# A hybrid decoder layer: the q, k and v projections as Strassen products over token halves

## The chip, the core and the metric

One core of a Trainium2 chip runs the whole program. It has a matmul engine (PE, with a separate weight load, PEld), three elementwise engines (VectorE or DVE, ScalarE or ACT, GpSimd or POOL), and SyncE (SP), which here issues nearly all transfers between DRAM and the core's two memories, SBUF and PSUM. Each engine executes its own instructions in order and waits for others by semaphores. The metric is device time in microseconds; less is better. The kernel before takes 2383.71 us, the median of three runs (2383.62 to 2387.13).

## What is computed

A decoder layer on x of 2048 tokens and 1024 channels, in float32. The normalised input h goes through one wide projection. One branch is a gated delta rule over chunks (its code is not touched). The other is causal attention in 12 combinations of 3 groups and 4 heads of 128 channels; the groups look at every token, every 4th or every 16th. Both branches are gated, projected, merged and added to x. What the change rewrites is the part from h to the three attention inputs, and the order of the attention blocks:

```python
h = rms_norm(x, norm_w[layer])
proj = h @ w_in[layer]
(dn_qkv, dn_z, dn_b, dn_a, swa_q, swa_k, swa_v, swa_z, gates) = jnp.split(proj, split_points, axis=-1)
...
sq = partial_rope(rms_norm(grp(swa_q), q_norm_w[layer][:, None, :]), cos, sin)
sk = partial_rope(rms_norm(grp(swa_k), k_norm_w[layer][:, None, :]), cos, sin)
sv = grp(swa_v)
for gi, (window, dilation) in enumerate(SWA_GROUPS):
    o_g, lse_g = dilated_window_attention(sq[:, :, gi], sk[:, :, gi], sv[:, :, gi], window, dilation)
```

Every float32 product is made of three: each operand is split into a rounded high part and the rest, its low part (`hh`, `hl` for h; `wh`, `wl` for weights), and high x high, high x low and low x high are added up in PSUM.

## The kernel before

**Data.** `hh` and `hl` stay in SBUF for the whole kernel, each [128 channels, 4 token groups of 512, 8 channel blocks, 512 tokens]. x is read twice, token-major for the row norms and channel-major (`xcol`) for the operand.

**Start.** `swa_first` (L368) loads the first unit's weights, clears `kq`, warms PE with 26 small matmuls and prepares the first 128 tokens of h; the other 15 pieces are prepared beside the first unit (`x_event`, `x_parts`).

**Units.** `swa_units` (L423) runs 12 units, one for each group and head, group 2 first. A unit projects 16 token blocks of 128 to 384 columns (q, k and v of its head). A block is one PSUM tile, 8 channel blocks x 3 matmuls at L238 to L240: 128 tokens are the loaded weights, 384 columns stream. A block is written in four quarters (`s_proj`); between them stand a third of an attention step (`att_slots`) and, from the block before, the normalisation (`s_norm`: square sums on ScalarE, the power -0.5 on GpSimd; `s_turn`: scaling on VectorE, rotation on GpSimd, the store to `rscr`). The next unit's weights are loaded and split from the seventh block on (`w384`).

**Attention.** 192 blocks wait in `self.att`, each with the step at which it starts. A step loads q, k, v of a block two steps ahead (`a_load`), transposes q and k (L290) and splits them into `kq`, then scores (L305 to L310), masks and takes the maximum (L312), exp (L317), transposes p (L324), multiplies by v (L332, L333) and stores to `oscr`. One block starts a step; a unit's blocks of groups 2 and 1 are added when the unit ends. What is left after the units is worked off beside the next matmuls by `att_background`, a third of a step every 6 matmuls.

**After.** `cunits` (L506) makes 36 column units for the other projections: 128 columns for all 2048 tokens, four PSUM tiles of 512 tokens, 24 matmuls each at L524 to L526. The first three (z) cover the rest of the attention; then come the delta rule and the final projections, which the change leaves alone.

**Order.** The engines' order is fixed by the code in the first part; from then on a scheduler places the instructions as it sees operands become ready, SP's too. Instructions that were written later can so stand earlier, the loads of weights above all.

## Time and profile before

| | |
|---|---|
| median of three runs | 2383.71 us |
| profiled execution, first to last instruction (span) | 2382.4 us |
| instructions in the profiled execution | 40700 |
| last matmul of the units (L240) | 1019.4 us |
| DMA over the span | 307.30 MB, 129 GB/s |

The span is the profiled execution's own time; 1.3 us lie between it and the median of the runs. A page of the profile gives each engine's busy time, the chain of work that ended last, and the costliest groups of instructions (line, engine, operation, output and inputs, count, busy us, mean ns of one, idle time before and what ended it). A matmul's duration includes its way through the array and overlaps the next one, so the cost of one in a row of many is the distance between two starts, which the timeline shows.

### The profile page before, as it was taken

How to read it: one execution, taken by the hardware profiler on the slowest of the kernel's cores; microseconds unless marked ns; L12 is line 12 of the kernel's file. 1: busy time of each engine (PE TensorE's matmuls, PEld its weight loads, DVE VectorE, ACT ScalarE, POOL GpSimd, SP SyncE). 2: the span in 40 equal slices, each digit the busy share in tenths (PEclk: the TensorE clock that was granted, in tenths of full speed). 3: DMA queues.
4: the chain of work that ended last, by engine and by line, in shares of the span. 5: the costliest groups of instructions: out<-in, count | busy, mean ns of one | idle time of the engine just before them, and what ended most of it. 6: DMA issues, size and time to landing. Idle time of an engine off the chain costs nothing.

```text
span 2382.4 us, 40700 instructions
## 1 busy us (share of the span) xinstructions
PE 2343.1 (98%) x13640; PEld 2133.7 (90%) x13640; DVE 1191.4 (50%) x2831; ACT 847.5 (36%) x3021; POOL 886.0 (37%) x1855
## 2 busy tenths in 40 slices
PE   8999999999999999999999999999999999999999
PEld 7899999999999999988878888888888878889988
DVE  5543344334334434344877775999344433454431
ACT  6433333344444434333666662111233313111110
POOL 6633333333333334310855671101233212433441
PEclk9999999999999999999999999999999999999999
DMA  8443344333333335233544443222577645554542
GB/s 283 158 116 111 107 123 121 95 103 112 110 97 112 108 91 128 86 91 92 142 121 130 116 115 116 69 73 75 193 209 203 182 151 157 164 178 156 149 140 75
DMA packets 378808, 307.30 MB, mean 129 GB/s; under 512 B 61352, under 2 KB 345320, under 8 KB 378216
## 3 DMA queue, kind: packets, MB, share of 16 engines
q1 hardware_dynamic: 378312, 304.64, 43.6%
q8 instruction: 108, 1.77, 0.3%
q14 instruction: 100, 0.82, 0.1%
q10 hardware_dynamic: 288, 0.07, 0.0%
HBM read 187.92 MB, written 116.69 MB: 128 GB/s over the span
## 4 chain that ended last, share of the span: by engine, by line
PE 85%; POOL 4%; DMA 4%; DVE 4%; ACT 2%; issue 2%; SPq 0%; POOLq 0%; ACTq 0%; DVEq 0%
PE mm L240 10%; PE mm L238 10%; PE mm L239 10%; PE mm L524 9%; PE mm L526 9%; PE mm L525 9%; PE mm L1054 2%; PE mm L1052 2%; PE mm L1053 2%; PE mm L1035 2%; PE mm L1037 2%; PE mm L1036 2%; PE po L333 2%; PE tp L290 2%; DMA gcb<-gcscr 1%
## 5 line engine op out<-in xcount | busy, mean ns | idle before, releaser
L238 PE MATMUL mm<-wh,hh 128*128 128x384 f32 (+1 forms) x1536 | 555.0, 361 | 6.3 <-ACT hh L131 2.9
L240 PE MATMUL mm<-wh,hl 128*128 128x384 f32 (+1 forms) x1536 | 519.7, 338 | 1.7 <-DVE hl L135 1.7
L239 PE MATMUL mm<-wl,hh 128*128 128x384 f32 (+1 forms) x1536 | 518.3, 337 | 0.7 <-DVE wl L79 0.6
L524 PE MATMUL mm<-hh,wh 128*128 128x512 f32 x1152 | 464.1, 403 | 0.0
L526 PE MATMUL mm<-hh,wl 128*128 128x512 f32 x1152 | 454.7, 395 | 0.0
L525 PE MATMUL mm<-hl,wh 128*128 128x512 f32 x1152 | 451.4, 392 | 0.0
L238 PEld LDWEIGHTS mm<-wh,hh 128*128 128x128 f32 x1536 | 290.2, 189 | 10.8 <-ACT wh L78 4.4
L239 PEld LDWEIGHTS mm<-wl,hh 128*128 128x128 f32 x1536 | 291.0, 189 | 1.7 <-DVE wl L79 1.1
L240 PEld LDWEIGHTS mm<-wh,hl 128*128 128x128 f32 x1536 | 289.3, 188 | 2.6 <-DVE hl L135 2.6
L526 PEld LDWEIGHTS mm<-hh,wl 128*128 128x128 f32 x1152 | 217.0, 188 | 46.9
L525 PEld LDWEIGHTS mm<-hl,wh 128*128 128x128 f32 x1152 | 217.4, 189 | 41.8
L524 PEld LDWEIGHTS mm<-hh,wh 128*128 128x128 f32 x1152 | 217.2, 189 | 42.0
L263 DVE SCALAR_TENSOR_TENSOR rec<-mm,st,wqk 128x128 f32<-128x128 f32 x384 | 116.7, 346 | 263.7 <-POOL st L255 244.2
L79 POOL TENSOR_TENSOR wl<-raw,wh 128x512 fp32r<-128x512 f32 (+1 forms) x73 | 104.6, 1445 | 382.3 <-ACT wh L78 382.0
L317 ACT ACTIVATE p<-sc,ol 128x128 f32<-128x128 f32 (+1 forms) x192 | 82.1, 428 | 316.8 <-DVE ol L315 273.0
L253 POOL TENSOR_SCALAR st<-st 128x2 f32<-128x2 f32 x192 | 38.0, 198 | 399.7 <-ACT rec L249 398.2
L249 ACT ACTIVATE rec<-mm 128x128 f32<-128x128 f32 x384 | 102.7, 273 | 185.0 <-PE mm L240 171.8
L1035 PE MATMUL mm<-oh,hh 128*128 128x256 f32 x512 | 143.9, 281 | 2.9 <-DVE gt L1039 2.9
L1037 PE MATMUL mm<-oh,hl 128*128 128x256 f32 x512 | 142.9, 279 | 0.0
L1036 PE MATMUL mm<-ol,hh 128*128 128x256 f32 x512 | 142.9, 279 | 0.0
L255 POOL TENSOR_TENSOR st<-st,mhalf 128x2 f32<-128x2 f32 x192 | 135.0, 703 | 16.0
L632 DVE SCALAR_TENSOR_TENSOR acc<-xr,cw,acc 128x512 f32<-128x512 f32 x144 | 122.4, 850 | 17.4 <-ACT acc L630 12.4
(244 smaller groups left out, 4332.0 us busy)
## 6 DMA issues: line engine op xcount, KB each, us to landing
rscr<-rec SPq DMA_DIRECT2D x192, 192.0 KB, 1.9
raw<-in_w_in_dram SPq DMA_DIRECT2D x138, 256.0 KB, 3.1
qk<-rscr SPq DMA_DIRECT2D x192, 128.0 KB, 2.2
gscr<-gt SPq DMA_DIRECT2D x64, 256.0 KB, 2.4
gt<-gscr SPq DMA_DIRECT2D x64, 256.0 KB, 3.5
oscr<-ol SPq DMA_DIRECT2D x192, 65.0 KB, 2.0
oc<-oscr SPq DMA_DIRECT2D x16, 780.0 KB, 5.3
v<-rscr SPq DMA_DIRECT2D x192, 64.0 KB, 2.0
```

What stands on the lines that cost most here:

```text
L238: nc.tensor.matmul(pr[:, :w], a, wh[:, k, :w], start=(k == 0), stop=False)
L239: nc.tensor.matmul(pr[:, :w], a, wl[:, k, :w], start=False, stop=False)
L240: nc.tensor.matmul(pr[:, :w], b, wh[:, k, :w], start=False, stop=(k == KT - 1))
L255: nc.gpsimd.tensor_tensor(out=st[:, 2:4], in0=st[:, 0:2], in1=self.mhalf[:, 0:2], op=ALU.pow)
L263: nc.vector.scalar_tensor_tensor(out=qk[:, j, :], in0=pr[:, j * P:(j + 1) * P], scalar=st[:, 2 + j:3 + j], in1=s["w"][2][:, j, :], op0=ALU ...
L524: nc.tensor.matmul(pr, wh[:, k, :], a, start=(k == 0), stop=False)
L525: nc.tensor.matmul(pr, wh[:, k, :], b, start=False, stop=False)
L526: nc.tensor.matmul(pr, wl[:, k, :], a, start=False, stop=(k == KT - 1))
L632: nc.vector.scalar_tensor_tensor(out=acc, in0=xr[:, j:j + 512], scalar=w[:, j:j + 1], in1=acc, op0=ALU.mult, op1=ALU.add)
L1035: nc.tensor.matmul(o, self.wbh[:, k, ms], oh[:, k, :], start=(k == b * 4), stop=False)
L1036: nc.tensor.matmul(o, self.wbh[:, k, ms], ol[:, k, :], start=False, stop=False)
L1037: nc.tensor.matmul(o, self.wbl[:, k, ms], oh[:, k, :], start=False, stop=(k == b * 4 + 3))
```

## The change

The projections are done for two token halves p of 1024 tokens. In a half, h is a 2 x 2 matrix of operands A (token half x channel half, each 512 x 512) and a pair of heads' weights a 2 x 2 matrix B (channel half x 256 columns). Strassen's method in Winograd's form makes the four blocks of the product from seven block products instead of eight, with the sums S1 to S4 of A and T1 to T4 of B. Eight operands (A and S) of one half, each high and low, fill `hh` and `hl`, but for A21, which no product uses: its place holds weights.

- `first_unit` prepares x, makes the sums on VectorE, splits them, and computes v of group 2 for all tokens in the plain way with 256 columns. All 16 operands go to DRAM (`opd`): those of half 1 (and A21) in pieces of 512 bytes a row as they are made, the others of half 0 by `save` in rows of 8 KB.
- 16 units follow (`self.seq`): 12 for q and k of two heads, four for v of a group. A unit is 7 products x 48 matmuls of 256 columns (L391 of the changed kernel). `evict` adds partial results held in SBUF, `consume` normalises (or stores, for v) two token blocks at a time. Where the half changes (after units 1, 6 and 12), each operand is replaced from DRAM after its last use; at the end the original layout of h is restored in the same way.
- Weights are loaded as B blocks; `w_sums`, `w_high`, `w_low` prepare a product's weights two products ahead, in a ring of four.
- A counter of six matmuls (a tick) times all of this. An attention step takes 4 ticks (`att_loop`); blocks are added as their units end, group 0 in two parts, for which each head loads and transposes one block again.
- PSUM and `rawp` are now allocated in two phases, with one buffer for the scores in the first. The mask step takes the scaled minimum, so one VectorE instruction a block falls away. In `cunits` the first unit takes its token groups in the order 2, 0, 1, 3.

```diff
+ORDER = [0, 4, 1, 5, 2, 6, 3, 7, 8, 12, 9, 13, 10, 14, 11, 15]
+OPS = ("A11", "A12", "A21", "A22", "S1", "S2", "S3", "S4")
+SLOT = {"A11": (2, 0), "A12": (2, 1), "A21": (3, 0), "A22": (3, 1), "S1": (0, 0), "S2": (0, 1), "S3": (1, 0), "S4": (1, 1)}
+HOME = {"S1": "A11", "S2": "A12", "S3": "A21", "S4": "A22"}
+PROD = (("A11", "a", True, "B11"), ("S2", "b", True, "T2"), ("A12", "a", False, "B21"), ("S3", "b", False, "T3"),
+        ("S1", "c", True, "T1"), ("A22", "b", False, "T4"), ("S4", "c", False, "B22"))
...
+    def slot(self, op):
+        n, h = SLOT[op]
+        return tuple(a[:, n, 4 * h:4 * h + 4, :] for a in (self.hh, self.hl))
...
+    def save(self, p, op):
+        for x, t in enumerate(self.slot(op)):
+            self.nc.sync.dma_start(self.opd_ap(p, op, x), t.bitcast(F32))
+
+    def restore(self, p, op, n, h):
+        for x, t in enumerate((self.hh, self.hl)):
+            self.nc.sync.dma_start(t[:, n, 4 * h:4 * h + 4, :].bitcast(F32), self.opd_ap(p, op, x))
...
+        if p or op == "A21":
+            for x, a in enumerate((h, l)):
+                self.nc.sync.dma_start(self.opd_ap(p, op, x, j), a.bitcast(F32))
...
+    def x_sums(self, m):
...
+        s1 = new("S1", a21, a22, ALU.add)
+        s2 = new("S2", s1, a11, ALU.subtract)
+        self.x_put(m, "S1")
+        new("S4", a12, s2, ALU.subtract)
+        self.x_put(m, "S2")
+        new("S3", a11, a21, ALU.subtract)
...
+    def x_put(self, m, op):
+        nc = self.nc
+        s = self.xsum.pop(op)
+        p, j = ORDER[m] // 8, ORDER[m] % 4
+        if p == 0:
+            h, l = (a[:, :, j * P:(j + 1) * P] for a in self.slot(op))
+        else:
+            h, l = self.xp.tile([P, 4, P], F32R, name="xh", bufs=4), s
+        nc.scalar.activation(h, s, AF.Copy)
+        nc.gpsimd.tensor_tensor(out=l, in0=s, in1=h.bitcast(F32), op=ALU.subtract)
+        if p:
+            nc.sync.dma_start(self.opd_ap(p, op, 0, j), h.bitcast(F32))
+            nc.sync.dma_start(self.opd_ap(p, op, 1, j), l)
...
+        for e in range(2):
+            self.ring.append(tuple(ap.tile([P, 4, 264], F32R, name=f"w{x}{e}", bufs=1) for x in "hl"))
+            self.ring.append(tuple(a[:, 3, 0:4, e * 256:(e + 1) * 256] for a in (self.hh, self.hl)))
...
+    def up_setup(self, up):
...
+        for j, nm in enumerate(("q_norm_w", "k_norm_w")):
+            nc.sync.dma_start(self.wqk[:, :, j, :], dr(self.i[nm], 0, [[0, P], [P, G], [1, P]]))
+        nc.sync.dma_start(self.rope, self.i["rope"])
...
+    def sp_setup(self, sp):
...
+        nc.sync.dma_start(self.mask, self.i["mask"])
         self.kq = sp.tile([P, 2, 3, P], F32R, name="kq", bufs=1)
         nc.vector.memset(self.kq[:, :, 0:2, :].bitcast(F32), 0.0)
...
+    def w_sums(self, gi):
...
+        if i == 1:
+            r[u, "T1"] = b11 = r.pop((u, "B11"))
+            sub(b11, r[u, "B12"], b11)
+            t2 = r[u, "T2"] = self.ap.tile([P, 4, 264], F32, name="wr", bufs=5)
+            sub(t2, r[u, "B22"], b11)
...
+    def w_ahead(self, gi):
...
+            if i == 5:
+                self.w_load(u + 1, "B11")
+                self.w_load(u + 1, "B12")
+            elif i == 6:
+                self.at(5, lambda: self.w_load(u + 1, "B22"))
+        if i == 0:
+            self.w_load(u, "B21")
...
+        self.w_sums(gi)
+        d = 2 if i in (1, 3, 5) else 0
+        self.at(d + 1, lambda: self.w_high(gi))
+        self.at(d + 3, lambda: self.w_low(gi))
...
-        for k in ks:
-            a, b = self.hh[:, t // 4, k, cs], self.hl[:, t // 4, k, cs]
-            nc.tensor.matmul(pr[:, :w], a, wh[:, k, :w], start=(k == 0), stop=False)
-            nc.tensor.matmul(pr[:, :w], a, wl[:, k, :w], start=False, stop=False)
-            nc.tensor.matmul(pr[:, :w], b, wh[:, k, :w], start=False, stop=(k == KT - 1))
...
+    def consume(self, u, tok, c, b, pr, add=None):
...
+        src, wait = pr, 0
+        if add is not None:
+            nc.vector.tensor_tensor(out=flat, in0=pr, in1=add, op=ALU.add)
+            src, wait = flat, 2
...
+                nc.scalar.activation(self.junk, src[:, j * P:(j + 1) * P], AF.Square, accum_out=st[:, j:j + 1])
+            nc.gpsimd.tensor_scalar(out=st[:, 0:4], in0=st[:, 0:4], scalar1=1.0 / P, scalar2=EPS,
+                                    op0=ALU.mult, op1=ALU.add)
+            nc.gpsimd.tensor_tensor(out=st[:, 4:8], in0=st[:, 0:4], in1=self.mhalf[:, 0:4], op=ALU.pow)
...
+                nc.vector.scalar_tensor_tensor(out=flat[:, s], in0=src[:, s], scalar=st[:, 4 + j:5 + j],
+                                               in1=self.wqk[:, g, j % 2, :], op0=ALU.mult, op1=ALU.mult)
...
+        self.at(wait + 6, scale)
+        self.at(wait + 8, turn)
...
+    def evict(self, u, i, b, pr):
...
+        if i == 0:
+            t = hold["p1", b] = self.up.tile([P, 512], F32, name="p1", bufs=2)
+            nc.scalar.activation(t, pr, AF.Copy)
+        elif i in (1, 3):
+            n = "u2" if i == 1 else "u3"
+            t = hold[n, b] = self.up.tile([P, 512], F32, name=n, bufs=2)
+            nc.vector.tensor_tensor(out=t, in0=pr, in1=hold["p1", b], op=ALU.add)
+        elif i == 2:
+            self.consume(u, 0, 0, b, pr)
+        else:
+            n, tok, c = {4: ("u3", 1, 1), 5: ("p1", 1, 0), 6: ("u2", 0, 1)}[i]
+            self.consume(u, tok, c, b, pr, hold.pop((n, b)))
...
+    def unit(self, u):
...
+        for i, (op, tgt, first, _) in enumerate(PROD):
+            gi = 7 * u + i
+            self.w_ahead(gi + 2)
+            if first:
+                acc[tgt] = [self.ps.tile([P, 512], F32, name="mm", bufs=4) for _ in range(2)]
+            ah, al = self.slot(op)
+            wh, wl = self.W.pop(gi)
+            for b in range(2):
+                pr = acc[tgt][b]
+                for jj in range(2):
+                    cs = slice((2 * b + jj) * P, (2 * b + jj + 1) * P)
+                    o = pr[:, jj * 256:(jj + 1) * 256]
+                    for k in range(4):
+                        mm = lambda x, y, **kw: nc.tensor.matmul(o, x, y, skip_group_check=True, **kw)
+                        mm(ah[:, k, cs], wh[:, k, :], start=first and jj == 0 and k == 0, stop=False)
+                        mm(ah[:, k, cs], wl[:, k, :], start=False, stop=False)
+                        mm(al[:, k, cs], wh[:, k, :], start=False, stop=(k == 3))
+                        if k % 2:
+                            self.hook()
+                self.evict(u, i, b, pr)
+            if nxt is None:
+                if op in HOME:
+                    self.restore(1 - p, HOME[op], *SLOT[op])
+                if i == 6:
+                    self.restore(p, "A21", *SLOT["A21"])
+            elif nxt != p:
+                self.restore(nxt, op, *SLOT[op])
...
+    def first_unit(self, pinned):
...
+            for m in range(1, 16):
+                t = 8 * m
...
+                    on(t - 18, lambda m=m: (self.x_stat(m), self.x_nat(m + 1)))
+                    on(t - 14, lambda m=m: self.x_diag(m))
+                on(t - 11, lambda m=m: event(m))
+                on(t - 7, lambda m=m: (self.x_high(m, 0), self.x_high(m, 1)))
+                on(t - 6, lambda m=m: (self.x_low(m, 0, nc.vector), self.x_low(m, 1, nc.gpsimd)))
+                if m % 2:
+                    on(t - 5, lambda m=m: self.x_sums(m))
+                    on(t - 1, lambda m=m: self.x_put(m, "S4"))
+                    on(t + 2, lambda m=m: self.x_put(m, "S3"))
+            on(80, lambda: [self.w_load(0, n) for n in ("B11", "B12", "B22", "B21")])
+            for j, op in enumerate(o for o in OPS if o != "A21"):
+                on(76 + 6 * j, lambda op=op: self.save(0, op))
...
+    def att_loop(self, ph):
+        if self.att_on:
+            self.att_slots(self.step, ph)
+            if ph == 2:
+                self.step += 1
+            self.at((1, 2, 1)[ph], lambda: self.att_loop((ph + 1) % 3))
...
-                                       scalar=-3e38, scale=1.0, op0=ALU.add, op1=ALU.max, accum_out=ol[:, 129:130])
-        nc.vector.tensor_scalar(out=ol[:, 128:129], in0=ol[:, 129:130], scalar1=-SCALE, scalar2=None, op0=ALU.mult)
+                                       scalar=3e38, scale=-SCALE, op0=ALU.add, op1=ALU.min, accum_out=ol[:, 128:129])
...
-        nc.scalar.activation(p[:, lo:hi], sc[:, 256 + lo:256 + hi], AF.Exp, bias=ol[:, 128:129], scale=SCALE,
+        nc.scalar.activation(p[:, lo:hi], sc[:, 256 + lo:256 + hi], AF.Exp, bias=ol[:, 128:129], scale=-1.0,
                              accum_out=ol[:, 129:130])
...
+    def att_add(self, h, g, items, step):
+        for u, has, pre in items:
+            at = max(step + 6, self.att[-1]["at"] + 1) if self.att else step + 6
...
+            self.att.append(dict(g=g, h=h, i=u, at=at, slot=self.aslot, pre=pre, prev=self.att[-1] if has else None))
...
+        self.scb = 1
+        self.seq = [(0, "qk", 2, (0, 1)), (0, "qk", 2, (2, 3)), (1, "qk", 2, (0, 1)), (1, "qk", 2, (2, 3)),
+                    (1, "v", 1, None), (1, "qk", 1, (0, 1)), (1, "qk", 1, (2, 3)),
+                    (0, "v", 1, None), (0, "qk", 1, (0, 1)), (0, "qk", 1, (2, 3)),
+                    (0, "v", 0, None), (0, "qk", 0, (0, 1)), (0, "qk", 0, (2, 3)),
+                    (1, "v", 0, None), (1, "qk", 0, (0, 1)), (1, "qk", 0, (2, 3))]
...
+        self.first_unit(pinned)
+        xst.close()
+        self.up_setup(pool(ust, "up"))
+        self.sp_setup(pool(sws, "sp", "right"))
+        with pinned(False):
+            self.att_on = True
+            self.at(1, lambda: self.att_loop(0))
+            for u in range(len(self.seq)):
+                self.unit(u)
+                self.att_ready(u)
+            self.att_on = False
+            self.flush()
+        ust.close()
+        ast.close()
+        psa.close()
+        pst = ExitStack()
+        self.ps = self.ctx.enter_context(tc.tile_pool(name="ps", bufs=2, space=PSUM, **tile_))
```

**VectorE at the passage to the units.** `kq` is the buffer of split q and k of the attention; `[waits DMAHW...]` names the transfers' semaphores. Before, its clearing is among the first instructions:

```order
L1212 UNCONDITIONAL_BRANCH
L60 MEMSET mhalf 128x8
L159 MEMSET kq 128x2x256
L88 MEMSET ones 128x128
L193 TENSOR_TENSOR wl<-raw,wh 128x384
```

Now it stands between the weight sums of unit 0 (L259; the first row of it makes T1 and T2, the next T3), and waits for two transfers; L282 behind it makes the low part of T2:

```order
L259 TENSOR_TENSOR wr<-wr 128x4x256 [waits DVE_49] x2
L235 MEMSET kq 128x2x256 [waits DMAHW1_49,DMAHW0_49]
L259 TENSOR_TENSOR wr<-wr 128x4x256
L282 TENSOR_TENSOR hl<-wr,hh 128x4x256 [waits Activation_49]
L366 TENSOR_TENSOR u_1853<-mm,p_1797 128x512 [waits PE_49,Activation_49]
L366 TENSOR_TENSOR u_1880<-mm,p_1823 128x512 [waits PE_49,Activation_49]
L259 TENSOR_TENSOR wr<-wr 128x4x256 [waits DVE_49]
L334 SCALAR_TENSOR_TENSOR rec<-mm,st,wqk 128x128 [waits PE_49,DMAHW5_49,Activation_49,Pool_49]
```

The clearing moved from the kernel's start to behind the work of the first unit, because the buffer lies where that unit's buffers lay.

**SP at the same place.** Before, the norm weights `wqk` and the rotation table are loaded among the first pieces of x:

```order
L102 DMA xc<-in_xcol_dram 128x1024
L97 DMA xt<-in_x_dram 128x1024 x2
L409 DMA wqk<-in_q_norm_w_dram 128x128
L409 DMA wqk<-in_k_norm_w_dram 128x128
L410 DMA rope<-in_rope_dram 128x512
```

Now they are issued behind the last stores of operands (`opd1S...`) and of v:

```order
L206 DMA opd1S_123<-xh 512x1x128
L207 DMA opd1S_124<-xsum 512x1x128
L500 DMA vs_92<-rec 128x512
L206 DMA opd1S_121<-xh 512x1x128
L207 DMA opd1S_122<-xsum 512x1x128
L226 DMA wqk<-in_q_norm_w_dram 128x3x128
L226 DMA wqk<-in_k_norm_w_dram 128x3x128
L227 DMA rope<-in_rope_dram 128x512
```

The loads moved behind 58 MB of other transfers.

**PE at the end of the units.** Before, the column units (L524) follow the last projection (L240) directly:

```order
L240 MATMUL mm<-wh,hl 128x384
L524 MATMUL mm<-hh,wh_13346 128x512
L525 MATMUL mm<-hl,wh_13346 128x512
L526 MATMUL mm<-hh,wl_13347 128x512
L524 MATMUL mm<-hh,wh_13346 128x512
```

Now attention (L523 to L565) and transposes of the delta rule's decay (L693, L746) stand between the last projection and the first column matmul (L659):

```order
L556 MATMUL tp<-ident,p 128x128 x2
L542 MATMUL sc<-kq 128x256
L543 MATMUL sc<-kq 128x256
L564 MATMUL po<-v,pT 128x128
L565 MATMUL po<-v,pT 128x128
L523 MATMUL tp<-ident,qk 128x128 x2
L659 MATMUL mm<-hh,wh_14446 128x512
L660 MATMUL mm<-hl,wh_14446 128x512
```

Three blocks of attention moved ahead of the column units, and of the 39 blocks left there 24 stand together further on, with 63 column matmuls among them (4 of 20 before, with 15).

535 lines of the change are left out of this document (260 added, 275 removed).

## The prediction

> **What bounds the kernel now.** I read the page first, then the PE timeline in three places, then the windows and the DMA view.
>
> ```profile
> span 2382.4 us, 40700 instructions
> PE 2343.1 (98%) x13640; PEld 2133.7 (90%) x13640; DVE 1191.4 (50%) x2831; ACT 847.5 (36%) x3021; POOL 886.0 (37%) x1855
> ...
> PE 85%; POOL 4%; DMA 4%; DVE 4%; ACT 2%; issue 2%; SPq 0%; POOLq 0%; ACTq 0%; DVEq 0%
> PE mm L240 10%; PE mm L238 10%; PE mm L239 10%; PE mm L524 9%; PE mm L526 9%; PE mm L525 9%; PE mm L1054 2%; PE mm L1052 2%; PE mm L1053 2%; PE mm L1035 2%; PE mm L1037 2%; PE mm L1036 2%; PE po L333 2%; PE tp L290 2%; DMA gcb<-gcscr 1%
> ```
>
> PE is busy 98% of the span and carries 85% of the chain that ended last; the projection lines L238 to L240 are 30% of it. The next rows say whether anything else ends last in that stage (columns: PE, PEld, DVE, ACT, POOL busy with instruction counts, granted clock, DMA share, GB/s).
>
> ```profile
> 0.00:60.00 60.00, 48.72 (x255) 46.04 (x256) 35.37 (x110) 38.60 (x101) 38.70 (x77) 0.91 0.86 282
> 60.00:110.00 50.00, 44.39 (x249) 42.32 (x248) 28.00 (x82) 24.88 (x87) 36.87 (x83) 1.00 0.51 166
> 110.00:1000.00 890.00, 888.69 (x5626) 882.11 (x5625) 350.00 (x1246) 347.31 (x1544) 339.55 (x1026) 1.00 0.38 109
> ```
>
> From 110 to 1000 us PE idles 1.3 us in 890, the others are under 40% busy, and DMA is at 0.38. So in this stage a matmul taken away is time won. In the first 110 us PE idles 11.3 + 5.6 = 16.9 us and DMA is already at 0.86: there, more transfers may cost.
>
> **Term 1, the matmuls.** A matmul's own duration overlaps the next one's, so I take start-to-start spacing.
>
> ```profile
> 600.25 0.34 PE L239 MATMUL mm<-wl,hh 128*128 128x384 f32 x1
> ...
> 601.98 0.34 PE L240 MATMUL mm<-wh,hl 128*128 128x384 f32 x1
> ...
> 40.11 0.34 PE L238 MATMUL mm<-wh,hh 128*128 128x384 f32 x1
> ...
> 42.04 0.34 PE L240 MATMUL mm<-wh,hl 128*128 128x384 f32 x1
> ...
> 2199.76 0.28 PE L1036 MATMUL mm<-ol,hh 128*128 128x256 f32 x1
> ...
> 2206.36 0.28 PE L1035 MATMUL mm<-oh,hh 128*128 128x256 f32 x1
> ```
>
> 384 columns: 10 steps from 600.25 to 601.98 give 173 ns, 11 from 40.11 to 42.04 give 175.5; I use 174. 256 columns, with the same kind of operands in the last stage: 56 steps in 6.60 us, 117.9 ns. Before: 12 units x 16 blocks x 24 = 4608 x 0.174 = 801.8 us. Changed: 768 in the first V unit and 16 x 7 x 48 = 5376, together 6144 x 0.1179 = 724.4 us. The eight columns for beta and decay ride on 384 matmuls in both. **-77 us.** The attention blocks keep their matmuls; four extra blocks, one a head, only transpose: 0.14 (599.85 to 599.99 under Term 3) and some 0.1 for the slower matmul behind them. **+1**.
>
> **Term 2, the stores of the split operands: the term that decides.** The change writes all 16 operands, high and low, to DRAM: 33.6 MB. The queue up to the last of them also holds x twice (16.8), two units' weights (4.2) and 15 V blocks (3.9): 58 MB ahead of the query and key norm weights, in SP's order. Two instructions wait for that. VectorE's clearing of `kq` waits for two DMA lanes, which I take for two among the last sixteen small stores (55.6 to 57.7 MB into the queue). Queued behind it on VectorE are T3's subtraction and the low part of T2, and PE waits for that low part in the second product of unit 0. The normalisation L334 waits for `wqk`, which stands right behind the stores; that lands about when the products after the first wait are done, so it is not counted again. How fast does the queue move?
>
> ```profile
> 10.00:20.00 10.00, 6.38 (x25) 5.52 (x25) 6.59 (x17) 6.33 (x13) 6.24 (x7) 0.66 1.07 357
> ...
> 1700.00:1900.00 200.00, 198.99 (x1333) 173.56 (x1333) 79.41 (x253) 68.56 (x267) 55.48 (x169) 1.00 0.68 194
> ...
> L79 DVE TENSOR_TENSOR wl<-raw,wh 128x512 fp32r<-128x512 f32 x66 | 45.8, 695 | 110.7 <-ACT wh L78 108.5 <-DMA oscr<-ol 2.1
> ```
>
> The busiest ten microseconds moved 357 GB/s at a share of 1.07, that is 334 at one. The stage at 1700 us, with many short rows like those in the small stores (512 B each), gives 194/0.68 = 285. The first 60 us gave 282. I take 334: 55.6 to 57.7 MB take 166 to 173 us, from 2 us on, so the wait ends at about 172, and clearing, subtraction and split (1.4 each for twice the 512 elements of L79, an estimate) add 3. Without the wait PE would be there at 16.9 (the idle time of today, kept) + 4.9 (warm-up matmuls, busy in the first row) + 816 x 0.118 + 1 = 119 us. **+56 us**; at 357 and the nearer store 42, at 285 and the farther one 88.
>
> The Trainium skill, "DMA: Bandwidth & Descriptors", section "Specifications", speaks against the change here: it gives an HBM limit of about 358 GB/s a core, and by it, as an estimate, the term would be 45 to 50. It also gives 435 GB/s as the fabric's ceiling; the trace has passed the first figure for some microseconds (the row under the rivals), so I don't take it for a wall.
>
> **Term 3, the pace inside the units.** A block of attention now has 24 matmuls of 118 ns (2.83 us) beside it, not 24 of 174.
>
> ```profile
> 599.85 0.38 PE L290 MATMUL tp<-ident,qk 128*128 128x128 f32 x2
> 599.99 0.42 PE L238 MATMUL mm<-wh,hh 128*128 128x384 f32 x1
> ...
> 605.42 0.42 PE L238 MATMUL mm<-wh,hh 128*128 128x384 f32 x1
> ...
> L249 ACT ACTIVATE rec<-mm 128x128 f32<-128x128 f32 x384 | 102.7, 273 | 185.0 <-PE mm L240 171.8 <-POOL rec L274 7.0 <-DMA rscr<-rec 4.6
> L78 ACT ACTIVATE wh<-raw 128x512 fp32r<-128x512 f32 x138 | 87.0, 633 | 70.6 <-PE mm L525 66.1 <-DMA raw<-in_w_in_dram 4.3 <-POOL hl L135 0.3
> L317 ACT ACTIVATE p<-sc,ol 128x256 f32<-128x256 f32 x108 | 51.2, 474 | 177.6 <-DVE ol L315 177.6
> L297 ACT ACTIVATE kq<-tp 128x256 fp32r<-128x256 f32 x128 | 49.3, 385 | 65.0 <-PE tp L290 64.5
> L298 DVE TENSOR_TENSOR kq<-tp,kq 128x256 fp32r<-128x256 f32 x128 | 54.3, 424 | 49.4 <-ACT kq L297 49.4
> L326 ACT ACTIVATE pT<-tp 128x256 f32<-128x256 f32 x108 | 41.6, 385 | 37.2 <-PE tp L324 37.2
> ```
>
> One step today is 5.43 us, of which 1.25 are attention on PE; it becomes 4.08. ScalarE then has per step four squares (0.27), exp (0.47 and its sum), two evictions (0.39) and half a weight rounding (1.27 for twice the 512 elements, an estimate): 3.1 of 4.08. Between the transposes and the score that uses them stand 12 matmuls and one transpose, 1.8 us, where 18 wide ones stood (3.1 us); the chain inside is 0.39 on ScalarE and 0.42 on VectorE with hand-offs. It fits unless another item is ahead on either engine. VectorE is over its time only in the last product of a unit (two adds, eight scalings, two weight sums and two blocks: about 8.9 us in 8.2). Nine units have both; I take 0.9 us each, **+8**; nothing at the low end (the 1.3 us in 890 of today), 36 if half of the 126 blocks there lose 0.6 us.
>
> **Term 4, the switches of halves.** Three times 14.7 MB come back, 44 us at 334 GB/s, in a unit of 40 to 57 us; each operand has a whole unit between its release and its next use. Weights and attention loads queue behind 2 MB pieces of 6 us. **+5** (0 to 15).
>
> **Term 5, from the units to the z columns.**
>
> ```profile
> 1019.39 0.34 PE L240 MATMUL mm<-wh,hl 128*128 128x384 f32 x1
> 1019.57 0.39 PE L524 MATMUL mm<-hh,wh 128*128 128x512 f32 x1
> 1019.79 0.40 PE L525 MATMUL mm<-hl,wh 128*128 128x512 f32 x1
> ...
> 1018.38 0.38 SPq L284 DMA_DIRECT2D v<-rscr  x1
> ...
> L255 POOL TENSOR_TENSOR st<-st,mhalf 128x2 f32<-128x2 f32 x192 | 135.0, 703 | 16.0
> L263 DVE SCALAR_TENSOR_TENSOR rec<-mm,st,wqk 128x128 f32<-128x128 f32 x384 | 116.7, 346 | 263.7 <-POOL st L255 244.2 <-DMA v<-rscr 15.5 <-DMA oscr<-ol 3.8
> L271 POOL TENSOR_TENSOR t<-rec,rope 128x64 f32<-128x64 f32 x192 | 64.8, 338 | 146.0 <-DVE rec L263 135.4 <-DMA qk<-rscr 6.4 <-DMA v<-rscr 2.6
> ...
> raw<-in_w_in_dram SPq DMA_DIRECT2D x138, 256.0 KB, 3.1
> ```
>
> Today the z matmuls follow without a gap, because their weights were loaded before. Now SP issues that load behind the last normalised block: add 0.7 (as L79), squares 1.1, power 0.9 for four columns, four scalings 1.4, eight rotations 2.4, some nine issues at 0.4, landing 3.1, rounding 0.6: 13.8 us and hand-offs of 1. Three blocks of attention (3.8 us) cover part: **+11** (6 to 15).
>
> **Term 6, the drain.**
>
> ```profile
> 1108.71 0.39 PE L333 MATMUL po<-v,pT 128*128 128x128 f32 x2
> ...
> 1118.38 0.39 PE L333 MATMUL po<-v,pT 128*128 128x128 f32 x2
> ```
>
> By the order, 39 blocks are left behind the units, not 20, and 24 of them, not 4, have only 2 to 4 z matmuls beside them. Those four took 9.67 us with 15 z matmuls of 0.22: 2.42 a block, 0.3 of it idle. 24 x 0.33 = **+8** (4 to 20). What follows is unchanged.
>
> **The sum:** -77 + 1 + 56 + 8 + 5 + 11 + 8 = +12 on the profiled 2382.4, so 2394; the median 2383.7 lies 1.3 above that span: **2396 us**. Low ends give -24, high ends +98.
>
> **The rivals.** *Faster: the stores run like the long transfers.* The DMA view of 1675 to 1710 us gives the rate in 40 slices:
>
> ```profile
> GB/s 274 26 0 0 0 0 165 160 134 444 502 393 449 412 468 393 468 431 393 487 342 337 286 28 0 0 45 238 239 325 301 353 347 207 209 244 302 369 355 237
> ```
>
> Here two transfers of 2 MB held about 440 for ten microseconds. Half of the new stores are long rows too. At 400 overall the wait ends at 146 instead of 172, Term 2 is 30, and with the other terms in the lower half (3, 2, 9, 6) the sum is -26: 2358. It decides from about 360 GB/s, where the sum passes zero with the other terms as forecast. Against it: the other half are 512 B rows, and the 285 above. *Slower: the pace of attention becomes the bound,* VectorE and ScalarE being late for each score by 0.3 us in 126 blocks: +38 for 8, 2426. For it the slack of 1.8 us instead of 3.1; against it ScalarE at three quarters. *The matmuls don't get shorter,* because a weight load is the limit at 256 columns:
>
> ```profile
> L1036 PEld LDWEIGHTS mm<-ol,hh 128*128 128x128 f32 x512 | 95.8, 187 | 0.3
> ```
>
> If each cost its 187 ns, 6144 x 0.069 = +424. The spacing of 117.9 with the same loads speaks against it.
>
> **How the numbers follow.** Forecast 0.53, faster rival 0.30, pace 0.15, weight loads 0.02. A measurement of this kernel can tell about 0.2%, 5 us. Of the forecast 0.10 and of the faster rival 0.03 lie within that: faster 0.27, same 0.13, slower 0.60. The forecast's own range is 2378 to 2430. The range given goes down into the faster rival and up past the pace rival, 2352 to 2450: below and above it I leave 0.1 each. As cases of both signs hold much, the sign is weak.
>
> **What would show it.** Term 1: L391 spaced 118 ns, PE busy about 75 us less. Term 2: PE idle for 40 to 90 us before unit 0's second or fifth product, released by VectorE, with DMA near a share of one from 60 to 170 us; if PE is through unit 0 by 160 us, the term is wrong and the kernel is faster. Term 3: idle at the scores, released by VectorE. Term 5: one gap before the first z matmul, released by ScalarE's rounding. Term 6: blocks 2.2 to 2.5 us apart. A gap in the units above 3 us that a restored operand ends would make Term 4 wrong.

## The result: 5.4% slower

| | before | changed |
|---|---|---|
| median of 4 runs | 2384.08 us | 2513.62 us (2512.80 to 2515.84) |
| ratio, 95% interval | | 1.0543 (1.0528 to 1.0557) |
| span of the profiled execution | 2382.4 us | 2513.9 us |

The forecast was 2396, with a range to 2450: the sign was right, the size wrong by 118 us. First the page of the changed kernel (same parts as those shown of before):

```profile
span 2513.9 us, 43806 instructions
...
PE 2330.1 (93%) x15184; PEld 2106.3 (84%) x15184; DVE 1389.9 (55%) x2882; ACT 959.6 (38%) x2976; POOL 1066.5 (42%) x1754
...
PE 58%; DMA 6%; POOL 5%; DVE 3%; ACT 3%; issue 2%; SPq 0%; POOLq 0%; ACTq 0%; DVEq 0%
```

PE is busy 13 us less than before (2330 for 2343), not some 75 less as forecast, and idle 184 us instead of 39. The chain that ended last has only 58% on PE (85% before); DMA has 6% and GpSimd (POOL) 5%, 4% each before. The shares listed add up to 77%, so the chain does not account for the whole span. The windows say where the time went. They are cut at the changed kernel's stages: first unit (two rows), the 16 units, the passage from the last product to the first column matmul, the rest; then before, cut at 110 us and at its last L240 (columns as in the prediction).

```profile
0.00:110.00 110.00, 80.00 (x540) 77.20 (x541) 62.53 (x135) 55.48 (x118) 56.14 (x63) 0.86 0.86 269
110.00:191.80 81.80, 39.29 (x289) 38.66 (x287) 23.55 (x51) 22.06 (x47) 25.16 (x23) 0.75 1.00 346
191.80:1080.80 889.00, 830.32 (x6755) 815.85 (x6756) 507.44 (x1261) 423.67 (x1458) 504.64 (x988) 0.97 0.57 178
1080.80:1109.70 28.90, 7.87 (x33) 5.23 (x32) 9.43 (x31) 6.71 (x28) 11.05 (x37) 0.59 0.83 236
1109.70:2513.90 1404.20, 1372.67 (x7573) 1169.36 (x7572) 786.89 (x1408) 451.70 (x1326) 469.50 (x646) 0.99 0.47 135
```

```profile
0.00:110.00 110.00, 93.11 (x502) 88.36 (x503) 63.37 (x191) 63.48 (x187) 75.57 (x160) 0.95 0.70 229
110.00:1019.50 909.50, 908.19 (x5752) 901.50 (x5751) 357.55 (x1273) 354.65 (x1574) 346.52 (x1048) 1.00 0.38 108
1019.50:2382.40 1362.90, 1341.83 (x7390) 1143.81 (x7388) 770.51 (x1368) 429.37 (x1260) 463.95 (x648) 1.00 0.46 135
```

The loss is in every stage: 72 us idle in the first unit, 59 in the units (1.3 before), 21 in the passage, 10 more than before in the rest. In the changed kernel the granted clock (the third number from the end) is under 1 in every stage, and lowest where the idle share is largest. The waits of PE in the changed kernel name the releasers (us in all, times, longest):

```profile
PE tp L140 <- ACT dg L136: 58.4, 11, 17.1
PE tp L556 <- ACT p L549: 19.2, 22, 4.4
PE mm L391 <- POOL wl L282: 15.2, 3, 5.2
PE tp L693 <- DVE s L721: 15.2, 1, 15.2
PE tp L823 <- DVE kT L772: 15.1, 5, 10.4
PE tp L523 <- DMA qk<-qks: 13.9, 8, 4.5
PE mm L391 <- ACT wh L275: 9.3, 1, 9.3
PE mm L391 <- POOL hl L282: 6.4, 2, 4.7
```

L140 spreads the norms of the next 128 tokens in the first unit; L556 and L523 are attention; L391 waits for weights (the 9.3 us stand ahead of unit 0's first product); L693 and L823 stand in the passage and behind the drain. The second product of unit 0, where the forecast had put its wait, does not appear.

### The profile page after: what moved, and what is told of

It is laid out like the page before. It is cut to its first block, busy times and chain, and to the rows that moved or that the text cites. A ratio compares the mean times of both kernels' runs of the same rounds, so it can differ in the third digit from the quotient of the medians.

```text
span 2513.9 us, 43806 instructions
## 1 busy us (share of the span) xinstructions
PE 2330.1 (93%) x15184; PEld 2106.3 (84%) x15184; DVE 1389.9 (55%) x2882; ACT 959.6 (38%) x2976; POOL 1066.5 (42%) x1754
## 4 chain that ended last, share of the span: by engine, by line
PE 58%; DMA 6%; POOL 5%; DVE 3%; ACT 3%; issue 2%; SPq 0%; POOLq 0%; ACTq 0%; DVEq 0%
PE mm L391 10%; PE mm L659 8%; PE mm L661 8%; PE mm L660 8%; PE mm L1189 2%; PE mm L1187 2%; PE mm L1188 2%; PE mm L1170 2%; PE mm L1172 2%; PE mm L1171 2%; DMA gcb<-gcscr 2%; DMA qk<-qks 2%; PE tp L523 1%; PE po L565 1%; POOL kql L863 1%
## 5 line engine op out<-in xcount | busy, mean ns | idle before, releaser
L659 PE MATMUL mm<-hh,wh 128*128 128x512 f32 x1152 | 466.9, 405 | 0.0
L391 PE MATMUL mm<-wh,hh 128*128 128x256 f32 x896 | 274.2, 306 | 9.3 <-ACT wh L275 9.3
L391 PE MATMUL mm<-wl,hh 128*128 128x256 f32 x896 | 259.4, 290 | 16.1 <-POOL wl L282 15.2
L391 PE MATMUL mm<-hh 128*128 128x256 f32 x896 | 270.1, 301 | 1.9 <-ACT hh L275 1.9
L391 PE MATMUL mm<-hl,hh 128*128 128x256 f32 x896 | 254.6, 284 | 6.4 <-POOL hl L282 6.4
L391 PE MATMUL mm<-wh,hl 128*128 128x256 f32 x896 | 259.3, 289 | 0.0
L391 PE MATMUL mm<-hh,hl 128*128 128x256 f32 x896 | 254.5, 284 | 0.0
L659 PEld LDWEIGHTS mm<-hh,wh 128*128 128x128 f32 x1152 | 218.6, 190 | 41.5 <-ACT wh L83 0.4
L391 PEld LDWEIGHTS mm<-wl,hh 128*128 128x128 f32 x896 | 176.7, 197 | 17.0 <-POOL wl L282 15.8
L391 PEld LDWEIGHTS mm<-wh,hh 128*128 128x128 f32 x896 | 177.2, 198 | 9.5 <-ACT wh L275 9.5
L391 PEld LDWEIGHTS mm<-hl,hh 128*128 128x128 f32 x896 | 172.6, 193 | 6.8 <-POOL hl L282 6.8
L391 PEld LDWEIGHTS mm<-wh,hl 128*128 128x128 f32 x896 | 175.9, 196 | 0.0
L391 PEld LDWEIGHTS mm<-hh 128*128 128x128 f32 x896 | 172.6, 193 | 2.1 <-ACT hh L275 2.1
L391 PEld LDWEIGHTS mm<-hh,hl 128*128 128x128 f32 x896 | 171.6, 192 | 0.0
```

The source lines that it names most:

```text
L391: mm = lambda x, y, **kw: nc.tensor.matmul(o, x, y, skip_group_check=True, **kw)
L659: nc.tensor.matmul(pr, wh[:, k, :], a, start=(k == 0), stop=False)
```

## Experiments

Each kernel is the changed kernel with the edit shown; its time is one run, to be held against 2513.6, whose runs differ by 3 us. The kernel before, run once beside each set, took 2383.4 to 2387.6, so a difference of under some 4 us is not told apart. Length of a unit: from its first matmul at L391 to that of the next unit.

**GpSimd: x1.** Low parts of the weights all on VectorE.

```diff
-        eng = eng or (self.nc.vector if i in (0, 2, 6) else self.nc.gpsimd)
+        eng = eng or self.nc.vector
```

> All low parts of the weights (L282) are made on VectorE instead of half of them on GpSimd. Theory 'GpSimd is full': in a q-k unit GpSimd has 8 powers and rotations of 4.0 us and about four low parts of 2.4 us, 42 us of work in a unit of 40 us without attention, so the weights come late in units 1, 2, 3 and 9 and SyncE's queue waits behind the late rotations. It expects PE's waits for L282 (21.6 us by GpSimd in all, and the half clock behind them) to go, and a shorter tail behind the last unit: 2514 falls by 25 to 40, to about 2480. Rival 'VectorE is as full': its four more low parts of 1.4 us a unit make the adds and scalings late, and the gain is under 10 us.

Measured 2505.7, 8 less. The groups of GpSimd from 192 to 1081 us show what fills it in the changed kernel (busy us, mean ns of one):

```profile
L329 POOL TENSOR_TENSOR st<-st,mhalf 128x4 f32<-128x4 f32 x94 | 97.4, 1036 | 7.8
L346 POOL TENSOR_TENSOR t<-rec,rope 128x64 f32<-128x64 f32 x184 | 76.3, 415 | 10.4 <-DVE rec L334 1.4
L282 POOL TENSOR_TENSOR wl<-wr,wh 128x1024 fp32r<-128x1024 f32 x32 | 76.3, 2384 | 107.8 <-ACT wh L275 57.2 <-DMA qk<-qks 23.3 <-DMA v<-vs 20.8
L347 POOL TENSOR_TENSOR t<-rec,rope 128x64 f32<-128x64 f32 x184 | 66.2, 360 | 0.0
L349 POOL TENSOR_TENSOR rec<-t,t 128x32 f32<-128x32 f32 x184 | 53.3, 290 | 0.0
L348 POOL TENSOR_TENSOR rec<-t,t 128x32 f32<-128x32 f32 x184 | 52.4, 285 | 14.4
L327 POOL TENSOR_SCALAR st<-st 128x4 f32<-128x4 f32 x94 | 27.6, 294 | 137.7 <-ACT junk L326 134.2
```

Eight times a q-k unit: a power (1.04 + 0.29) and two rotations of 1.35, 4.0 us; with four low parts of 2.4 that is 41.8 us in a unit whose matmuls take 39.8. Units 1, 2, 3 and 9 fell from 47.6, 52.0, 53.1 and 56.2 us to 44.9, 49.2, 51.8 and 51.6, 11 us in all, and PE no longer waits for GpSimd's L282. So GpSimd's low parts did hold PE up, but the time fell by only 8 us, not by 25 to 40, and that is within the rival's "under 10". The rotations stayed, and a 4.1 us wait at the first weights of unit 2 appeared.

**Returns: x2.** No operand comes back where the half changes.

```diff
-            elif nxt != p:
-                self.restore(nxt, op, *SLOT[op])
```

> Leaves out the three times that operands come back from DRAM where the half changes (the last restore, of h, stays), so all units compute with the operands of half 0. Theory 'restores': units 6, 7, 12 and 13 are 66, 59, 69 and 65 us long against 51 to 58 for units without restores, so about 38 us are the restores', and 3 to 8 more in units 1 and 2: about 2470. Rival 'pace': attention at one block in four ticks is late by itself and the long units only hold its catching up; then less than 12 us go.

Measured 2478.9, 35 less. Windows of units 6, 7, 12 and 13 in the changed kernel, then the same units without returns:

```profile
493.10:559.30 66.20, 55.31 (x436) 53.21 (x435) 37.02 (x105) 29.59 (x116) 39.73 (x85) 0.95 0.85 294
559.30:618.30 59.00, 53.37 (x437) 52.20 (x436) 30.93 (x85) 21.18 (x65) 23.26 (x41) 0.97 0.67 206
832.00:901.00 69.00, 62.59 (x485) 59.87 (x482) 37.71 (x105) 35.72 (x130) 40.14 (x85) 0.95 0.84 283
901.00:966.00 65.00, 58.67 (x481) 57.49 (x479) 33.57 (x85) 27.58 (x77) 22.06 (x41) 0.97 0.60 186
```

```profile
487.40:541.60 54.20, 51.78 (x437) 50.82 (x435) 36.69 (x105) 29.47 (x116) 39.58 (x85) 1.00 0.49 147
541.60:595.00 53.40, 51.22 (x438) 50.67 (x435) 32.02 (x85) 21.05 (x65) 23.92 (x41) 1.00 0.57 167
808.50:867.50 59.00, 58.38 (x485) 56.69 (x482) 37.66 (x105) 35.78 (x130) 38.94 (x85) 1.00 0.44 133
867.50:925.90 58.40, 57.28 (x482) 56.20 (x479) 32.97 (x85) 27.53 (x78) 23.48 (x41) 1.00 0.52 155
```

The work is the same, the four units are 34 us shorter and at full clock. The rival of pace falls.

**Stores: x3 and y1.** x3 stores half 0 during unit 0:

```diff
-            for j, op in enumerate(o for o in OPS if o != "A21"):
-                on(76 + 6 * j, lambda op=op: self.save(0, op))
...
             gi = 7 * u + i
+            if u == 0:
+                self.at(2, lambda op=op: self.save(0, op))
```

> The 14.7 MB of half 0 are stored during unit 0, each operand at its product, instead of during the first unit. Theory 'the first unit is bound by transfers': at 334 GB/s 14.7 MB are 44 us; unit 0 starts at about 150 instead of 192 and units 0 and 1, whose transfers fill 0.42 and 0.64 of the time, lengthen by under 8: about 2476. Rival 'the chain of x': each piece of x has one buffer, so its load, its sum of squares and its scale follow one another, whatever else the queue holds; then unit 0 starts at 180 or later and the time falls by under 12.

Measured 2484.7, 29 less; unit 0 starts at 165 us, between the two forecasts, and units 0 and 1 are no longer for it (42.0 and 47.0 for 43.7 and 47.6). y1 drops all stores and returns of operands:

```diff
-        if p or op == "A21":
-            for x, a in enumerate((h, l)):
-                self.nc.sync.dma_start(self.opd_ap(p, op, x, j), a.bitcast(F32))
...
-        if p:
-            nc.sync.dma_start(self.opd_ap(p, op, 0, j), h.bitcast(F32))
-            nc.sync.dma_start(self.opd_ap(p, op, 1, j), l)
...
-                    self.restore(1 - p, HOME[op], *SLOT[op])
+                    pass
                 if i == 6:
-                    self.restore(p, "A21", *SLOT["A21"])
-            elif nxt != p:
-                self.restore(nxt, op, *SLOT[op])
+                    pass
...
-                on(76 + 6 * j, lambda op=op: self.save(0, op))
+                pass
```

> Leaves out every store and every return of the split operands (the half switches, and h at the end): nothing of the 33.6 MB goes to DRAM or comes back. Theory 'the traffic of the operands is the bulk of the loss': unit 0 starts near 125 us instead of 192, units 6, 7, 12 and 13 are as short as in the run without returns (54, 53, 59, 58), so about 65 + 38 = 103 go and the time is 2405 to 2415; what stays of the loss, 20 to 30, is GpSimd's lateness, the passage to the column units and the drain. Rival 'the chain of x' (one buffer for each piece of x): unit 0 starts at 150 or later and the time is over 2430.

Measured 2424.3: the operands' traffic costs 89 us, 47 of them ahead of unit 0, which starts at 144.8. That is neither 125 nor 150. PE is at unit 0's second product at 151.5, where the forecast without a wait had 119: 32 us of the late start have another cause. In y1 PE idles 29.4 us ahead of unit 0, where the forecast kept the 16.9 of the kernel before; 24.4 of them are for the norms of the next piece of x. ScalarE, which makes them, waits for the loads of x, which has one token-major buffer (PE's waits in the whole run, ScalarE's from 60 to 145 us):

```profile
PE tp L140 <- ACT dg L136: 24.4, 12, 3.8
ACT xt L129 <- DMA xt<-in_x_dram: 13.4, 4, 4.1
```

And PE is busy 115.4 us there, with 768 matmuls that take 91 at 118.6 ns and 4.9 of warm-up: the granted clock was about 0.9. How the stores delay PE in the changed kernel is told by the waits of VectorE and ScalarE from 60 to 192 us:

```profile
DVE xsum L182 <- DMA opd1S<-xsum: 37.4, 4, 13.0
DVE xc L146 <- PE tp L140: 21.0, 5, 6.8
ACT xh L164 <- DVE xc L146: 16.6, 7, 9.0
ACT xh L203 <- DMA opd1S<-xh: 12.1, 3, 4.9
```

The sums S have three buffers, and the low part is stored from the buffer itself; it is free only when the store has landed. VectorE stands at L182, and the scaling of the next piece of x (L146) behind it. ScalarE waits for that scaling and then for a buffer of high parts (`xh`) that a store still holds; behind both, in its order, stands the norm (`dg`), for which PE waits up to 17 us.

**A second piece of x: z2.**

```diff
-            self.xt[m] = self.xp.tile([P, D], F32, name="xt", bufs=1)
+            self.xt[m] = self.xp.tile([P, D], F32, name="xt", bufs=2)
...
-                l = self.xp.tile([P, 4, P], F32R, name="xl", bufs=4)
+                l = self.xp.tile([P, 4, P], F32R, name="xl", bufs=3)
...
-                    on(t - 18, lambda m=m: (self.x_stat(m), self.x_nat(m + 1)))
+                    on(t - 18, lambda m=m: (self.x_stat(m), self.x_nat(m + 2)))
```

> A second buffer for the token-major piece of x, loaded one piece earlier (room for it from one fewer buffer of low parts and a narrower warm-up). Theory 'chain of x': without any store unit 0 still started at 145 and not at 119, PE waiting 24 us for the scale of the next piece, which waits for a load that is issued only when the piece before has been read. It expects unit 0 to start 15 to 30 us earlier, about 2490. Rival 'the stores set the pace here': with them in the queue an earlier load takes the room of a store, and unit 0 starts within 8 us of 192.

Measured 2509.6; unit 0 starts at 183.7, 8 us earlier, at the rival's edge. With the second buffer ScalarE's wait for x is gone, but PE still waits 55.8 us at L140 (58.4 in the changed kernel): the stores hold the same place. The second buffer without stores, and more buffers for the sums and the high parts, were not tried.

**Two waits one behind the other: y2, z1, w1.** y2 loads attention four steps ahead, z1 has more buffers for the stored block result, w1 has both.

```diff
-            if "qk" not in a and (d == 0 or (d == -2 and which == 1)):
+            if "qk" not in a and (d == 0 or (d == -4 and which == 1)):
...
-        ol = a["ol"] = sp.tile([P, 130], F32, name="ol", bufs=3)
+        ol = a["ol"] = sp.tile([P, 130], F32, name="ol", bufs=8)
```

(With the first edit qk has 5 buffers, v 8, and a block starts 8 steps behind its unit.)

> The attention's loads are issued four steps ahead instead of two (two more buffers for q-k and for v). Theory 'latency': in units 6, 7, 12 and 13 the loads land late because each stands behind 1 MB pieces of operands, 7.4 us in the median where others take 2.5, about the two steps that they are ahead; four steps cover it and the four units fall to within 4 us of 54, 53, 59 and 58: 20 to 35 less, about 2485. Rival 'rate': the transfers are full there (share 0.84) and a load that is issued earlier only waits longer: under 10 less.

> Eight buffers instead of three for ol, the block's result that is stored to oscr. Theory 'the store holds the buffer': during the returns VectorE's mask step waits for an ol whose store has not landed (27.8 us of waits for oscr<-ol from 440 to 960 us, 47.3 with loads issued earlier), and everything behind it on VectorE waits with it. It expects units 6, 7, 12 and 13 to fall from 66, 59, 69 and 65 by 5 to 9 us each, 20 to 35 in all, to about 2485. Rival 'loads': the loads of q and k are as late as before and end the same steps; under 8 less.

> Both edits of the attention's transfers at once: loads four steps ahead and eight ol buffers. Theory 'two waits one behind the other': alone each edit gained nothing, since PE then waited 27.5 us for loads (with more ol) or 34.9 us for p (with earlier loads); with both, units 6, 7, 12 and 13 fall from 66, 59, 69 and 65 to within 4 us of 54, 53, 59 and 58, about 2480. Rival 'rate': 14.7 MB of returns and the attention's own rows fill the transfers of these units, whoever waits; under 10 less.

Measured 2529.6, 2512.0 and 2502.2. PE's waits in units 6 and 7 (493 to 620 us), in this order: the changed kernel, y2, z1, w1:

```profile
PE tp L523 <- DMA qk<-qks: 7.7, 5, 3.7
PE tp L556 <- ACT p L549: 7.2, 6, 4.4
```

```profile
PE tp L556 <- ACT p L549: 15.5, 7, 4.4
```

```profile
PE tp L523 <- DMA qk<-qks: 13.7, 6, 3.9
PE tp L556 <- ACT p L549: 1.1, 1, 1.1
```

```profile
PE tp L556 <- ACT p L549: 5.1, 3, 2.8
PE tp L523 <- DMA qk<-qks: 4.2, 3, 1.5
```

One wait taken away, the other holds the whole sum. With both edits the four units take 60, 54, 62 and 59 us, 24 less, although unit 6 still moves 293 GB/s at a share of 0.83: late landing set their length, not the rate. Behind p stands the mask step on VectorE, which waits for the store of ol (in y2 27.3 us in these units):

```profile
DVE sc L545 <- DMA oscr<-ol: 27.3, 7, 6.8
```

Of the 24 us only 11 reach the time. Behind the first column matmul w1 takes 12 us more (1416.1 for 1404.2), as y2 does (1416.5): blocks start two steps later, two more of them are left (some 3 us of work), and PE idles 4 to 5 us more there. What makes up the rest of the 12 is not settled.

**The passage and the drain: y3, w2, x4, w3.** y3 lets attention run on:

```diff
+            for _ in range(40):
+                self.hook()
             self.att_on = False
```

> Attention goes on for 40 ticks (ten blocks) behind the last unit, instead of stopping there until the column units begin. Theory 'PE has nothing to do there': the 29 us from the last product to the first column matmul hold ten blocks that otherwise stand in the drain, each worth its 1.25 us of PE time, so the time falls by 8 to 14, to about 2502. Rival 'SyncE's queue': the loads of these blocks stand behind the last stores of q and k, which wait for GpSimd's rotations; the blocks wait as well, the gap grows by what they take, and the time stays within 5 us.

Measured 2509.6, 4 less and so within the rival's 5. Eight more blocks ran in the passage, which grew from 29 to 42 us, and the rest shrank by 18. w2 takes the last unit's rotations to VectorE:

```diff
-            G = nc.gpsimd
+            G = nc.vector if u == 15 else nc.gpsimd
```

> Only the last unit's rotations run on VectorE instead of GpSimd. Theory 'GpSimd's backlog': behind the last product GpSimd still has four powers and rotations to do, until 1096, and SyncE's queue (the stores, then the loads of attention and of the column units' weights) stands behind them; the first column matmul starts 8 to 12 us earlier behind the last product (29 us in the kernel as given), and the time falls by as much. Rival 'SyncE's own queue and the landing': under 4.

Measured 2511.7, within the rival's 4. The passage takes 24 us instead of 29, 5 less where the theory had 8 to 12: the rotations are part of it, and not most of it. x4 puts six column units ahead of the delta rule:

```diff
-        first, rest = zu[:3], zu[3:] + gu
+        first, rest = zu[:6], zu[6:] + gu
...
-        self.cunits(first + du + rest, {3: open_dn, 15: lambda: self.at(9, start_inverse)}, tail)
+        self.cunits(first + du + rest, {6: open_dn, 18: lambda: self.at(9, start_inverse)}, tail)
```

> Six column units instead of three stand ahead of the delta rule, so that fewer of the 39 blocks of attention left run without column matmuls beside them. Theory 'uncovered blocks': the fourth stretch of 96 column matmuls takes 74 us where before took 30; with 16 more blocks beside column matmuls about 16 x 1.1 us go, about 2495. Rival 'cover is only moved': the three column units are missing beside the delta rule, and the time stays within 8 us.

Measured 2511.3, within the rival's 8. The longest wait for `kT` at the delta rule's start did fall, from 10.4 to 4.6 us, and the part behind the first column matmul from 1404.2 to 1398.2; in the whole time so little does not show. w3 shortens the attention step:

```diff
-            self.at((1, 2, 1)[ph], lambda: self.att_loop((ph + 1) % 3))
+            self.at((1, 1, 1)[ph], lambda: self.att_loop((ph + 1) % 3))
```

> An attention step takes three ticks of six matmuls instead of four, so the queue of blocks empties earlier and about 20 blocks are left behind the units instead of 39. Theory 'the drain': the 24 blocks that stand together there cost more than beside products, and the passage behind them has lost its column matmuls (10 us of wait for kT): 8 to 17 less, about 2502. Rival 'pace of attention' (forecast at 0.15): with 18 matmuls for a block VectorE and ScalarE are late for each score, and the time rises by 5 or more.

Measured 2551.0, 37 more. The part behind the first column matmul did shrink, by 29 us (1374.8), but with the blocks that moved out of it the units grew by 68 us. By the block count 14 blocks moved, some 18 us of work. PE waits for p 39.1 us in all, for 19.2 in the changed kernel. Unit 5, into which no operand returns, idles 2.9 us of 59.2, and unit 12, with returns, 15.3 of 86.0. So at 18 matmuls a block the pace costs something by itself and more where operands return; at 24 it costs next to nothing by itself (units 5 and 14 idle under 0.3 us).

**The returns in another queue: v1.**

```diff
-            self.nc.sync.dma_start(t[:, n, 4 * h:4 * h + 4, :].bitcast(F32), self.opd_ap(p, op, x))
+            self.nc.scalar.dma_start(t[:, n, 4 * h:4 * h + 4, :].bitcast(F32), self.opd_ap(p, op, x))
```

> The returned operands are issued by ScalarE instead of SyncE; nothing else. The Trainium skill, page 'DMA: Bandwidth & Descriptors', section 'Queues, rings and completion order', says that each DMA engine takes turns between the queues it has work for. By theory 'place in one queue' the attention's loads and stores then pass the 1 MB pieces, and units 6, 7, 12 and 13 fall from 66, 59, 69 and 65 by 20 to 30 in all, without more buffers: about 2487. Rival 'rate': the transfers are as full as before, under 8 less. Rival 'ScalarE stands': ScalarE, in order, waits for PE's last use of each operand and for free transfer lanes ahead of its own work, and the units get longer.

Measured 2529.3, 16 more: the rival that ScalarE stands. Unit 6 took 69.4 us for 66.2 and the last unit 63 for 57. ScalarE's waits from 493 to 570 us of this kernel, which hold its unit 6, have a row that the changed kernel's unit 6 hasn't:

```profile
ACT pT L558 <- DMA oscr<-ol: 8.2, 1, 8.2
```

The row fits ScalarE standing in front of its own work for a transfer; that this makes all 16 us is not shown. The turns between queues that the Trainium skill names ("DMA: Bandwidth & Descriptors", "Queues, rings and completion order") can't be seen in these runs.

**Sums: y4, z3, w4, v2.** y4 is x1, x3, y2 and y3 together; z3 has z1 and z2 for y2; w4 has all of them and w2; v2 adds v1.

> All the edits that computed the reference together: low parts on VectorE, half 0 stored during unit 0, loads four steps ahead, attention running on behind the last unit. If the losses are separate places, the gains add: 10 + 29 and what the two runs beside this one gain alone; by the theories of latency and of an idle PE that is 2425 to 2450, by their rivals 2465 to 2475. If one place hides another, less than their sum.

> Low parts on VectorE, half 0 stored during unit 0, attention running on behind the last unit, and the two edits beside it (eight ol buffers, a second piece of x); loads two steps ahead. The earlier sum of edits gave 2474. By 'the store holds the buffer' and 'chain of x' together about 45 less, 2430; by their rivals 2460 to 2475.

> All edits that keep the result together (low parts on VectorE, half 0 stored during unit 0, second piece of x, loads four steps ahead, eight ol buffers, attention running on, the last rotations on VectorE). Where the losses are separate, 2465 less what the first two runs of this set gain: 2425 to 2440 by their theories, 2455 to 2465 by their rivals. In no case under 2390: some 20 us of the first unit, the return of 14.7 MB three times and the drain stay.

> The last combination (2440) with the returns issued by ScalarE as well. If place in the queue is what is left of the returns' price in units 6, 7 and 2 (5 + 1 + 8 us) and at the end, 2428 to 2437; if ScalarE stands for the returns, over 2445.

Measured 2474.4, 2464.8, 2440.1 and 2459.1: y4 and z3 as their rivals had it, w4 at the edge of its theories, v2 as if ScalarE stands. w4 regains 73.5 of the 130 us; it is still 2.4% over the kernel before, which took 2383.4 beside it. None beat it. Its edits alone (x1, x3, z2, w1, y3, w2) add up to 58: some of the waits hid others. In w4 the returns' units are 59, 55, 59 and 60 us.

## Why the prediction was wrong, term by term

| term | forecast | measured | from |
|---|---|---|---|
| 1 matmuls | -77 | -73 | 6144 x 0.1186 (rows below) for 801.8 |
| 2 stores | +56 | +82 | unit 0's second product starts at 201.2, not 119; the rest of the unit takes 34, as forecast |
| 3 pace in the units | +8 | +44 | units 1 to 15 without returns (x2): 807.5, less 15 x 39.8, less 167 for attention |
| 4 returns | +5 | +38 | units 1 to 15 with returns: 845.4 |
| 5 passage | +11 | +25 | 29.0 less three blocks (3.8) |
| 6 drain | +8 | +21 | 1404.2 for 1362.8, less 16 blocks x 1.25 that moved there |

With 1 for the four extra blocks that is +138, and the spans differ by 131.5. The 119 is too low by some of the 6 us between them: it leaves out the transposes of x's norms and the matmuls at a low clock that the kernel before pays as well (0.95 in its first 110 us). The rest is not placed. (Attention in the units: 14 blocks cost 51.2 - 39.8 us in unit 5 and 57.8 - 39.8 in unit 14; 64 blocks of group 2 and 89 others make 167.)

**Term 1 was right in the spacing.** In the changed kernel's timeline seven steps take 0.83 us, 118.6 ns each:

```profile
462.10 0.28 PE L391 MATMUL mm<-hh,hl 128*128 128x256 f32 x1
...
462.93 0.28 PE L391 MATMUL mm<-hh 128*128 128x256 f32 x1
```

That PE's busy time fell by 13 us and not by 75 is no fault of this spacing: ahead of unit 0 alone PE is busy 119.3 us (80.0 + 39.3) for 96 us of matmuls and warm-up at full clock.

**Term 2** had the right traffic: the two rows of the first unit make 110 x 269 + 81.8 x 346 = 57.9 MB, the 58 of the forecast, and nearly the right rate at a share of one, 346 for 334. The step that failed is "PE waits for that low part in the second product of unit 0": the first unit itself stood, at buffers that a store had not yet released. The share of 1.00 came only after 110 us at 269 GB/s, so 58 MB took 190 us and not 172. Without stores PE is at the second product at 151.5, so they cost 50 us of the 82, a little less than the 56 forecast; the other 32 were put at nothing. The rate of 346 held for 80 us is under the limit of about 358 that the Trainium skill gives ("DMA: Bandwidth & Descriptors", section "Specifications"). By the forecast's own bytes that limit gives, as an estimate, 41 to 47 us, not the 45 to 50 worked out there. The bursts of 440, on which the faster rival rested, did not last. Of those 32 us y1 shows 12.5 as idle time beyond the 16.9, for x's single buffer, and most of the others as matmuls at a low clock; z2 got 8 us of the whole back.

**Term 3** failed at "VectorE is over its time only in the last product of a unit". GpSimd's time was never added up, and so put at nothing, though the rows of its power, its rotation and the order's L282 were at hand. Units 1, 2, 3 and 9 make 33 of the 44 us; x1 shows 11 of them as the low parts'. That the rest is the rotations is argued from the sum of 41.8 us, not shown by a run. The other 11 us are near what PE still waits for p in the units of x2 (9.8 us in 12 waits, none over 1.3): what the forecast priced at 8 was there, at about that size.

**Term 4** rested on "each operand has a whole unit between its release and its next use". That was true, and PE never waited for an operand. What failed is the price of the next step, that attention's loads "queue behind 2 MB pieces of 6 us": 5 us for all three switches. These loads are only two steps ahead, and in the same queue stand attention's stores, whose three buffers are free only on landing. y2, z1 and w1 show the two waits, one behind the other.

**Term 5** had the right first links and the wrong lengths, and the wait stood elsewhere. GpSimd had four powers and rotations to do, until 1096, and SP, in order, stood behind them. VectorE then stood until an attention load landed, 5.9 us later, and PE's long wait ended at a transpose of the delta rule and not, as forecast, at ScalarE's rounding; the loads of the z weights were issued only at 1105.5. The rows are SP's stores and next loads, then PE's wait:

```profile
1091.33 5.21 SPq L350 DMA_DIRECT2D qks<-rec  x3
1096.64 0.77 SPq L516 DMA_DIRECT2D qk<-qks  x1
```

```profile
1102.81 0.42 PE L693 MATMUL tp<-ident,ab 128*64 128x128 f32 x1 [15.17 <-DVE s L721]
```

**Term 6** priced the drain and not what follows: 63 column matmuls stand between the last blocks, so none is left to cover the delta rule's start, and PE waits 10.4 us there for `kT` where the longest such wait was 2.1. With more cover (x4) it is 4.6. The rest of the 13 us that the forecast missed is not taken apart.

**No term** had the clock; what it cost is spread over the rows of the table. In unit 1 a wait of 4.9 us is followed by 23 steps of 213 ns instead of 118:

```profile
257.84 0.58 PE L391 MATMUL mm<-wl,hh 128*128 128x256 f32 x1 [4.91 <-POOL wl L282]
258.22 0.41 PE L391 MATMUL mm<-wh,hl 128*128 128x256 f32 x1
...
263.13 0.32 PE L391 MATMUL mm<-wl,hh 128*128 128x256 f32 x1
263.28 0.28 PE L391 MATMUL mm<-wh,hl 128*128 128x256 f32 x1
```

That is 2.2 us on top. The Trainium skill says so in "TensorE: Matmul & The Clock Gate", "Part 1: The HAM clock gate": an idle window of about 3.4 us brings half clock, a busy one full clock. This wait agrees. The rows of the kernel before showed it too (a clock of 0.91 in the first 60 us, where PE idled 11.3), but the forecast let every wait cost its own length.

The faster rival fell with Term 2; the pace rival, at 24 matmuls a block, with x2, though at 18 (w3) the pace begins to cost.
